# A transformer layer on one core: other scratch for block 2's squares, other slots for norms, late sums and output sums

## The chip, the cores and the metric

The kernel runs on one core of a Trainium2 chip. TensorE (PE) multiplies matrices and transposes, VectorE (DVE), ScalarE (ACT) and GpSimd (POOL) do the element work, and all transfers are issued from one queue, SyncE's (SP). The metric is the device time of one execution in microseconds; the median of several runs counts.

## The reference

The reference is one layer (`DEPTH` is 1, so only the first mixer runs) over a sequence of 2048 tokens of width 1024 in float32. The mixer is stick-breaking attention:

```python
def stick_breaking_mixer(h, w_qkv, w_o):
    qkv = (h @ w_qkv).reshape(b, s, 3, N_HEADS, HEAD_DIM)
    for q0 in range(0, s, SB_BLOCK):
        z = einsum('bthd,bshd->bhts', q[:, q0:end], k[:, :end]) * scale
        sp = where(mask, softplus(z), 0.0)
        rest = cumsum(sp, axis=3, reverse=True)
        a = exp(where(mask, z - rest, -inf))
        outs.append(einsum('bhts,bshd->bthd', a, v[:, :end]))
    return o @ w_o

def reference(x, c, ada_w, ada_b, norm_g, ffn_w_in, ffn_w_out, sb_w_qkv, sb_w_o, ...):
    mod_all = einsum('bd,lde->lbe', silu(c), ada_w) + ada_b[:, None]
    sh_m, sc_m, gt_m, sh_f, sc_f, gt_f = split(mod_all, 6)
    h = rms_norm(x, norm_g[0]) * (1 + sc_m) + sh_m
    x = x + gt_m * rms_norm(stick_breaking_mixer(h, ...), norm_g[1])
    h = rms_norm(x, norm_g[2]) * (1 + sc_f) + sh_f
    y = (silu(g) * u) @ ffn_w_out          # g, u = split(h @ ffn_w_in)
    return x + gt_f * rms_norm(y, norm_g[3])
```

The six vectors of `mod_all` are numbered 0 to 5 below (`seg`): shift, scale and gate of the mixer, then of the feed-forward part.

## The kernel before

**Numbers.** A float32 operand is split into a high part (rounded to a shorter format) and a low part (the rest), and a product is made of three matmuls (`mm3`, lines 190 to 194): high by high, high by low, low by high.

**Order.** The instructions of PE, ScalarE, VectorE and GpSimd run in the order in which the program writes them down. Transfers are put in order by the compiler's scheduler. All buffers come from pools with a fixed number of places under a tag: `ht` 5 (normed blocks), `qt` 3, `kt` 7, `v` 7, `wraw` 2, `qkn` 2, `tmp` 4; in PSUM `zps` 3 (scores), `tps` 2 (transposed weights), `accps` 3 under the tag `acc`. A new tile takes a place that is free, and its first writer waits until the last user of the place is done.

**Projections.** The tokens are four blocks of 512, the 16 heads eight pairs. A step (p, b) projects block b for head pair p: keys (t = 1), queries (t = 0), values (t = 2), each as eight slices over the width (k = 0 to 7), one slice being an `mm3`. `project(at)` is a generator that yields after each slice. `STEPS` begins with (0, 0), then (1, 0), whose results are parked in memory, then (0, 1), (0, 2), (0, 3), which are steps 2, 3 and 4. Steps 0 and 1 are computed ahead, in the lead-in written out by hand.

**Attention.** A unit is (pair, head, query block, key block), and each unit has four slots s. In every slot the program writes down one piece of each stage, with a delay in slots: scores `z` (line 588), sigmoids (605, 607), the scan that breaks the sticks (617, 622) and its product on GpSimd (629), the transposes `t` (639), their split into high (649) and low (655), the weighing of the values `o` (667), and some slices of the projections beside them. `project_to` sets how many: 18 slices are written before slot 0, and the projections then run ahead of the units.

**Norms of the first pair's blocks.** While head pair 0 is projected, each block is normed for the first time and stored for the other pairs. For block 2, `x_square` (line 328, through `rms_scale`, line 183) squares each of four tiles of 128 tokens on ScalarE and keeps only the sum; the squares themselves go to a scratch tile `xj` that nobody reads. `x_scale` (340) scales the rows on VectorE, `x_turn` (366) transposes them on PE, one eighth of the width at a time. Blocks 1 and 3 are loaded transposed (`xc`, line 325): `x_spread` and `x_share` bring the row factors into one tile, and `scale_cols` (376 on VectorE, 380 on GpSimd) multiplies by them. `modulate` then makes the high and the low part of a column tile (387 to 401). `first_norm(b, k)` does all this for eighth k of block b, and at odd k stores the finished pair (line 428). `X_AT` says in which slice the squares, scalings and loads are written; `NORM_AT` and the line below say the same for the norms:

```python
NORM_AT = [(2, 2), (2, 4), (2, 6)]      # eighths 0, 1, 2 of the next block, in the values product
first_norm(b, k + (4 if b == 1 else 3)) # the others, in the keys product of the block's own step
```

**Late modulation.** Segments 2 to 4 of `mod_all` are computed beside the attention by the generator `late_modulation`: from slot 120 on it is advanced every second slot. For each segment and each half it loads four chunks of weights into `wraw`, adds them up on VectorE (`aacc`), waits three steps (`settle`), takes an `acc` bank for the result `ap` and sums over the partitions on PE: one matmul by ones for a gate (line 293), four small products for a shift or scale (241). Three steps later (one for a shift or scale) VectorE reads the result (296, 249, 254). For a gate, a tile `gr` in `wraw` takes the constants (292) and goes out as rows (298). Segment 5 goes through the same function in the feed-forward part, with other tags.

**Output projection.** The two parts of each attention output are loaded (`o_load`), added (`o_add`, line 1082, on GpSimd for block 0 and on VectorE for the others) and split (`o_prep`). For block 0 this is written into the slots of the last pair.

The rest (output projection, second norm, feed-forward part) is not touched, but for segment 5 of the late modulation.

Of the kernel before, what the change touches and what calls it, by code (L numbers as in the profile page):

```python
# [9 lines left out]
F32 = mybir.dt.float32  # L10
F32R = mybir.dt.float32r
AF = mybir.ActivationFunctionType
ALU = mybir.AluOpType
# [3 lines left out]
P = 128  # L17
D = 1024
S = 2048
KC = D // P  # L20
# [3 lines left out]
BT = 512  # L24
# [26 lines left out]
BUFS = {  # L51
    "ht": 5, "whl": 4, "qt": 3, "kt": 7, "v": 7, "aT": 4, "qkn": 2, "wraw": 2,
    "tmp": 4, "w": 3, "a": 10,
}
# [35 lines left out]
    (3, 0, 1): [("share", 3)],  # L90
}

NORM_AT = [(2, 2), (2, 4), (2, 6)]

LAST_HELD = 30

# [24 lines left out]
def hybrid_trunk_kernel(  # L121
# [18 lines left out]
    nc = tc.nc  # L140
# [49 lines left out]
    def mm3(acc, lhs, rhs, first, last, **kw):  # L190

        nc.tensor.matmul(acc, lhs[0], rhs[0], start=first, stop=False, **kw)  # L192
        nc.tensor.matmul(acc, lhs[0], rhs[1], start=False, stop=False, **kw)  # L193
        nc.tensor.matmul(acc, lhs[1], rhs[0], start=False, stop=last, **kw)  # L194


    att = Places(ctx, tc)
    zps = ctx.enter_context(tc.tile_pool(name="zps", bufs=3, space=PSUM))
    tps = ctx.enter_context(tc.tile_pool(name="tps", bufs=2, space=PSUM))
    accps = ctx.enter_context(tc.tile_pool(name="accps", bufs=3, space=PSUM))  # L200
# [55 lines left out]
            g_eff[:, which, ks], sc, 1.0, gc[:, which, ks], op0=ALU.add, op1=ALU.mult  # L256
        )

    def late_modulation(segs, tag, n, ahead, waits, pool, ptag, acc_tag="tmp", rows_tag="wraw", settle=3, pace=1):

        chunks = [(seg, half, k0) for seg in segs for half in range(2) for k0 in range(0, KC, n)]
        loaded = []

        def load():
            if len(loaded) < len(chunks):
                loaded.append(ada_load(*chunks[len(loaded)], n, tag, BUFS[tag]))

        for _ in range(ahead):
            load()
        for at, (seg, half, k0) in enumerate(chunks):  # L270
            if ahead == 0 or at == 0:
                if ahead == 0:
                    load()
                for _ in range(waits):
                    yield
            if k0 == 0:
                acc = att.tile([P, BT], F32, name=f"aacc{seg}_{half}", tag=acc_tag, bufs=BUFS[acc_tag])
            for i in range(n):
                ada_add(acc, loaded[at], k0, i, k0 + i == 0)
                for _ in range(pace):  # L280
                    yield
            if ahead:
                load()
            if k0 + n < KC:
                continue
            for _ in range(settle):
                yield
            ps = pool.tile([P, BT], F32, name=f"ap{seg}_{half}", tag=ptag)
            if seg in (2, 5):
                g = seg // 3  # L290
                rows = att.tile([P, 2, BT], F32, name=f"gr{g}_{half}", tag=rows_tag, bufs=BUFS[rows_tag])
                nc.sync.dma_start(rows, gate_consts[g : g + 1, half].to_broadcast((P, 2, BT)))
                nc.tensor.matmul(ps, ones, acc, start=True, stop=True)
                for _ in range(3):
                    yield
                nc.vector.tensor_tensor(rows[:, 0], ps, rows[:, 0], op=ALU.add)
                nc.vector.tensor_tensor(rows[:, 0], rows[:, 0], rows[:, 1], op=ALU.mult)
                nc.sync.dma_start(gate_rows[g, :, half * BT : (half + 1) * BT], rows[:, 0])
            else:
                ada_cols([acc], ps, half)  # L300
                yield
                sl = slice(4 * half, 4 * half + 4)
                ada_done(seg, ps[:, sl], 1, sl)
            yield
# [3 lines left out]
    x_places = {}  # L308
# [19 lines left out]
    def x_square(b, i):  # L328
        junk = x_tiles[b, i]
        if b == 0:  # L330
            junk = x_norm[b, i] = att.tile([P, D], F32, name=f"xn{b}_{i}", tag="kt", bufs=BUFS["kt"])
        elif b == 2:
            junk = att.tile([P, D], F32, name=f"xj{b}_{i}", tag="wraw", bufs=BUFS["wraw"])
        x_rstd[b, i] = rms_scale(att, x_tiles[b, i], f"n0_{b}_{i}", junk=junk)

    def x_scale(b, i):
# [113 lines left out]
    def project(at):  # L450

        p, b = STEPS[at]
# [3 lines left out]
        nb = STEPS[at + 1][1] if at + 1 < len(STEPS) and STEPS[at + 1][0] == 0 else None  # L456
# [4 lines left out]
        def product(t):  # L461
            if begun:
                if at == 0 and t != 2:
                    first_norm(1, 2 + (t == 0))
                return first_acc[p, t]
            w = weights[p, t]
            acc = accps.tile([P, BT], F32, name=f"pj{p}_{b}_{t}", tag="acc")
            ahead = b == NB - 1 and p + 1 < NPAIR
            for k in range(KC):
                if t == 1:  # L470
                    if p == 0:
                        first_norm(b, k + (4 if b == 1 else 3))
                    if k in (3, 5) and waiting:
                        waiting.pop(0)()
                for what, *which in X_AT.get((at, t, k), []):
                    x_do[what](*which)
                if (t, k) in NORM_AT:
                    first_norm(nb, NORM_AT.index((t, k)))
                if ahead and k == 0:
                    load_weights(p + 1, t)  # L480
                if ahead and k == 6:
                    split_weights(p + 1, t)
                mm3(acc, (w[0][:, k], w[1][:, k]), (h[k][:, 0], h[k][:, 1]), k == 0, k == KC - 1)
                yield
            return acc

# [11 lines left out]
        n = split((yield from product(1)), "k")  # L498
# [13 lines left out]
        n = split((yield from product(0)), "q")  # L512
# [14 lines left out]
        acc = yield from product(2)  # L527
        tag = "w" if early else "tmp"
# [152 lines left out]
    rows, sums = {}, {}  # L681
# [267 lines left out]
    products(1, 6)  # L949
    products(0, 7)  # L950
    products(1, 7)
    late = late_modulation((2, 3, 4), "wraw", 2, 0, 3, accps, "acc")


    tasks = []
# [122 lines left out]
    def o_add(b, k):  # L1078
        parts = o_parts.pop((b, k))
        o = att.tile([P, BT], F32, name=f"of{b}_{k}", tag="tmp", bufs=BUFS["tmp"])  # L1080
        eng = nc.vector if b else nc.gpsimd
        eng.tensor_tensor(o, parts[:, 0], parts[:, 1], op=ALU.add)
        o_sum[b, k] = o

    def o_prep(b, k):
# [129 lines left out]
    for s in range(4 * len(units) + last):  # L1215
# [565 lines left out]
```

## Time and profile before

| what | value |
|---|---|
| median of 3 runs | 2841.5 us (2839.93 to 2845.77) |
| the profiled execution, its own time | 2840.45 us |
| its span from first to last instruction | 2838.2 us |
| mean granted TensorE clock | 0.998 |
| PE, VectorE, ScalarE, GpSimd busy | 2798.2, 2022.4, 1630.7, 1282.5 us |
| moved by DMA | 521.03 MB, mean 184 GB/s |

The span is what the profile's lines are measured in; the execution's own time is 2.25 us longer. Engines work in order, so an engine that waits holds up everything written down behind the waiting instruction. In a line of a timeline, the number in brackets is the idle time just before it, with what ended it. A granted clock of 1.00 is full speed of TensorE. In the lists of waits the numbers are the sum, the count and the longest.

### The profile page before, as it was taken

The numbers are of one execution on the slowest core, as the hardware profiler recorded it, in microseconds if no ns is written. First come the engines' busy times: TensorE is split into PE (matmuls) and PEld (weight loads), VectorE is DVE, ScalarE is ACT, GpSimd is POOL, SyncE is SP. The second block draws the span as 40 slices with busy tenths as digits, with TensorE's granted clock in tenths as the row PEclk, the third lists the DMA queues.
The fourth block names the chain that finished last, engine by engine and source line by source line (L and its number), as shares of the span: only waits on it lengthen the run. The fifth ranks groups of instructions, "written<-read, shape, count | busy, mean of one in ns | idle before, by whom it ended". The sixth has DMA issues, their size and how long they took to land.

```text
span 2838.2 us, 41766 instructions
## 1 busy us (share of the span) xinstructions
PE 2798.2 (99%) x13821; PEld 2331.5 (82%) x13821; DVE 2022.4 (71%) x2833; ACT 1630.7 (57%) x3271; POOL 1282.5 (45%) x2032
## 2 busy tenths in 40 slices
PE   9899999999999999999999999999999999999998
PEld 7688888888888888887888888888888888888887
DVE  7788888888888888888866766655775665123376
ACT  5787777787787877877645533333433333322243
POOL 1575666676576655657411222221222222544454
PEclk9999999999999999999999999999999999999999
DMA  9774556656665635546288644334453334545575
GB/s 378 275 226 164 186 163 220 212 179 226 193 210 187 214 115 178 196 134 231 85 304 308 207 138 152 123 94 160 137 178 108 112 108 164 192 140 155 180 226 187
DMA packets 239785, 521.03 MB, mean 184 GB/s; under 512 B 22481, under 2 KB 108497, under 8 KB 222674
## 3 DMA queue, kind: packets, MB, share of 16 engines
q1 hardware_dynamic: 239570, 518.38, 56.2%
q8 instruction: 109, 1.79, 0.3%
q14 instruction: 106, 0.87, 0.1%
HBM read 351.04 MB, written 118.49 MB: 165 GB/s over the span
## 4 chain that ended last, share of the span: by engine, by line
PE 88%; DVE 4%; issue 2%; DMA 2%; ACT 2%; POOL 1%; SPq 0%; DVEq 0%; POOLq 0%; ACTq 0%
PE s L192 9%; PE s L193 9%; PE s L194 9%; PE z L588 8%; PE o L667 8%; PE t L639 8%; PE pj L192 5%; PE pj L194 5%; PE pj L193 5%; PE o L194 5%; PE o L193 5%; PE o L192 5%; PE y L194 2%; PE y L192 2%; PE y L193 2%
## 5 line engine op out<-in xcount | busy, mean ns | idle before, releaser
L629 POOL TENSOR_TENSOR a<-a,w 128x512 f32<-128x512 f32 (+3 forms) x640 | 622.1, 972 | 218.9 <-DVE w L622 128.6
L622 DVE TENSOR_TENSOR_SCAN w<-z,c,begin 128x512 f32<-128x512 f32 x384 | 489.2, 1278 | 83.7 <-ACT z L607 62.0
L192 PE MATMUL s<-r,l 128*128 128x512 f32 x1232 | 481.4, 391 | 1.5 <-ACT p L1456 0.9
L194 PE MATMUL s<-r,l 128*128 128x512 f32 x1232 | 479.6, 389 | 0.0
L193 PE MATMUL s<-r,l 128*128 128x512 f32 x1232 | 479.4, 389 | 0.0
L605 ACT ACTIVATE a<-z 128x512 f32<-128x512 f32 (+3 forms) x640 | 347.1, 542 | 170.0 <-PE z L588 137.3
L667 PE MATMUL o<-aT,v 128*128 128x512 f32 (+3 forms) x1280 | 385.3, 382 | 0.1
L655 DVE TENSOR_TENSOR aT<-t,aT 128x512 fp32r<-128x512 f32 (+3 forms) x640 | 358.4, 593 | 24.3 <-ACT aT L649 23.7
L588 PE MATMUL z<-kt,qt 128*128 128x512 f32 (+3 forms) x1280 | 363.6, 365 | 0.0
L649 ACT CAST aT<-t 128x512 fp32r<-128x512 f32 (+3 forms) x640 | 313.9, 533 | 73.6 <-PE t L639 63.5
L607 ACT ACTIVATE z<-z 128x512 f32<-128x512 f32 (+3 forms) x640 | 344.8, 539 | 0.0
L1520 POOL TENSOR_TENSOR one<-p,p 128x512 f32<-128x512 f32 x44 | 70.6, 1606 | 574.5 <-issue 321.8
L192 PE MATMUL pj<-ht,w 128*128 128x512 f32 x768 | 309.3, 403 | 5.4 <-issue 1.4
L639 PE MATMUL t<-begin,a 128*128 128x128 f32 x2176 | 295.1, 273 | 13.3 <-DVE aT L655 12.0
L639 PEld LDWEIGHTS t<-begin,a 128*128 128x128 f32 x2176 | 255.2, 140 | 63.4 <-DVE aT L655 14.2
L193 PE MATMUL pj<-ht,w 128*128 128x512 f32 x768 | 301.7, 393 | 0.9 <-DVE ht L767 0.2
L194 PE MATMUL pj<-ht,w 128*128 128x512 f32 x768 | 301.9, 393 | 0.0
L192 PEld LDWEIGHTS s<-r,l 128*128 128x128 f32 x1232 | 231.2, 188 | 51.2 <-ACT p L1456 1.7
L194 PEld LDWEIGHTS s<-r,l 128*128 128x128 f32 x1232 | 231.2, 188 | 48.8 <-DVE l L1374 0.4
L193 PEld LDWEIGHTS s<-r,l 128*128 128x128 f32 x1232 | 231.3, 188 | 48.0 <-issue 0.5
L617 DVE TENSOR_TENSOR_SCAN w<-z,begin 128x128 f32<-128x128 f32 (+3 forms) x256 | 208.6, 817 | 76.9 <-ACT z L607 65.5
L588 PEld LDWEIGHTS z<-kt,qt 128*128 128x128 f32 x1280 | 230.9, 189 | 37.5 <-DVE w L617 0.2
(181 smaller groups left out, 4871.5 us busy)
## 6 DMA issues: line engine op xcount, KB each, us to landing
ht<-h_s SPq DMA_DIRECT2D x108, 1024.0 KB, 8.3
wi<-in_win SPq DMA_DIRECT2D x86, 512.0 KB, 3.9
qt<-qn SPq DMA_DIRECT2D x124, 256.0 KB, 4.8
ol_qt<-act_s SPq DMA_DIRECT2D x56, 512.0 KB, 3.7
act_s<-S SPq DMA_DIRECT2D x66, 256.0 KB, 4.0
br<-in_wout SPq DMA_DIRECT2D x66, 256.0 KB, 3.3
h_s<-ht SPq DMA_DIRECT2D x16, 1024.0 KB, 9.0
o_s<-os SPq DMA_DIRECT2D x128, 128.0 KB, 2.6
```

The source lines that it names most:

```text
L192: nc.tensor.matmul(acc, lhs[0], rhs[0], start=first, stop=False, **kw)
L193: nc.tensor.matmul(acc, lhs[0], rhs[1], start=False, stop=False, **kw)
L194: nc.tensor.matmul(acc, lhs[1], rhs[0], start=False, stop=last, **kw)
L588: nc.tensor.matmul(z[:, :n], q[:, e, part, r * P : (r + 1) * P], k[:, e, :n], start=part == 0, stop=part == 1,)
L605: nc.scalar.activation(a[:, :n], z[:, :n], AF.Sigmoid, scale=QK_SCALE)
L607: nc.scalar.activation(z[:, :n], z[:, :n], AF.Sigmoid, scale=-QK_SCALE)
L622: nc.vector.tensor_tensor_scan(rest[:, rev], left[:, rev], begin[:, :BT][:, rev], initial=carries[r], op0=ALU.mult, op1=ALU.bypass,)
L629: nc.gpsimd.tensor_tensor(a[:, :n], a[:, :n], rest[:, 1 : n + 1], op=ALU.mult)
L639: nc.tensor.transpose(pt[:, rb * P : (rb + 1) * P], weighed[i, rb][:, j * P : (j + 1) * P], ident)
L649: nc.scalar.copy(hl[:, 0, t0:], pt[:, t0:])
L655: nc.vector.tensor_tensor(hl[:, 1, t0:], pt[:, t0:], f32(hl[:, 0, t0:]), op=ALU.subtract)
L667: nc.tensor.matmul(acc[:, t0:], lhs, hl[:, part, t0:], start=sc == qb and j == 0 and part == 0, stop=sc == 0 and j == 3 and part == 1,)
```

## The change

Five edits. (1) The four squares of block 2 write to one tile under the tag `v`, taken at the first of them, in place of four tiles under `wraw`. (2) The norms of blocks 2 and 3 are written in other slices: the first in the queries product of the step before, then four in its values product, and the last three in the keys product of the block's own step. Block 1 keeps its slices. (3) Late sums: the result is made only when the last slice written is 2, 3 or 4 of its product (segments 2 to 4), and VectorE reads it in the same step. (4) The tile for a gate's rows and the transfer of its constants come before the settling steps. (5) The sums of block 0's output parts go from GpSimd to VectorE.

```diff
-NORM_AT = [(2, 2), (2, 4), (2, 6)]
+NORM_AT = {
+    None: [], 1: [],
+    2: [(0, 6), (2, 0), (2, 2), (2, 4), (2, 6)],
+    3: [(0, 4), (0, 7), (2, 2), (2, 4), (2, 6)],
+}
+
+NORM_IN_KEYS = {1: {0: 4, 1: 5, 2: 6, 3: 7}, 2: {0: 5, 1: 6, 3: 7}, 3: {0: 5, 1: 6, 3: 7}}
...
+    slice_at = [0]
...
-def late_modulation(..., settle=3, pace=1):
+def late_modulation(..., settle=3, pace=1, inside=None):
...
+            g = seg // 3
+            if seg in (2, 5):
+                rows = att.tile([P, 2, BT], F32, name=f"gr{g}_{half}", tag=rows_tag, bufs=BUFS[rows_tag])
+                nc.sync.dma_start(rows, gate_consts[g : g + 1, half].to_broadcast((P, 2, BT)))
             for _ in range(settle):
+                yield
+            while inside and slice_at[0] not in inside:
                 yield
             ps = pool.tile([P, BT], F32, name=f"ap{seg}_{half}", tag=ptag)
             if seg in (2, 5):
-                g = seg // 3
-                rows = att.tile([P, 2, BT], F32, name=f"gr{g}_{half}", tag=rows_tag, bufs=BUFS[rows_tag])
-                nc.sync.dma_start(rows, gate_consts[g : g + 1, half].to_broadcast((P, 2, BT)))
                 nc.tensor.matmul(ps, ones, acc, start=True, stop=True)
-                for _ in range(3):
-                    yield
                 nc.vector.tensor_tensor(rows[:, 0], ps, rows[:, 0], op=ALU.add)
...
             else:
                 ada_cols([acc], ps, half)
-                yield
                 sl = slice(4 * half, 4 * half + 4)
                 ada_done(seg, ps[:, sl], 1, sl)
...
         elif b == 2:
-            junk = att.tile([P, D], F32, name=f"xj{b}_{i}", tag="wraw", bufs=BUFS["wraw"])
+            if i == 0:
+                x_places["junk"] = att.tile([P, D], F32, name=f"xj{b}", tag="v", bufs=BUFS["v"])
+            junk = x_places["junk"]
...
                     if p == 0:
-                        first_norm(b, k + (4 if b == 1 else 3))
+                        first_norm(b, NORM_IN_KEYS[b].get(k, KC))
...
-                if (t, k) in NORM_AT:
-                    first_norm(nb, NORM_AT.index((t, k)))
+                if (t, k) in NORM_AT[nb]:
+                    first_norm(nb, NORM_AT[nb].index((t, k)))
...
                 mm3(acc, (w[0][:, k], w[1][:, k]), (h[k][:, 0], h[k][:, 1]), k == 0, k == KC - 1)
+                slice_at[0] = k
                 yield
...
-    late = late_modulation((2, 3, 4), "wraw", 2, 0, 3, accps, "acc")
+    late = late_modulation((2, 3, 4), "wraw", 2, 0, 3, accps, "acc", inside=range(2, 5))
...
-        eng = nc.vector if b else nc.gpsimd
-        eng.tensor_tensor(o, parts[:, 0], parts[:, 1], op=ALU.add)
+        nc.vector.tensor_tensor(o, parts[:, 0], parts[:, 1], op=ALU.add)
```

More of the change, by code (lines that the diff above doesn't have):

```diff
@@ L257, in ada_done, with late_modulation @@
         )
-    def late_modulation(segs, tag, n, ahead, waits, pool, ptag, acc_tag="tmp", rows_tag="wraw", settle=3, pace=1):
+    slice_at = [0]
+    def late_modulation(segs, tag, n, ahead, waits, pool, ptag, acc_tag="tmp", rows_tag="wraw", settle=3, pace=1, inside=None):
         chunks = [(seg, half, k0) for seg in segs for half in range(2) for k0 in range(0, KC, n)]
```

## The prediction

> **What bounds the kernel now.** I read the page first.
>
> ```profile
> span 2838.2 us, 41766 instructions
> PE 2798.2 (99%) x13821; PEld 2331.5 (82%) x13821; DVE 2022.4 (71%) x2833; ACT 1630.7 (57%) x3271; POOL 1282.5 (45%) x2032
> ```
>
> TensorE (PE) is the bound: it is busy for all but 40.0 us of the span, and the change takes no matmul away. So the only things to be had are idle time on PE and time in which it runs at a lower clock. I then looked for both where the edited code runs: PE's waits by window, and the granted clock by window.
>
> Slices are written (step, product, k) as in the code: one slice is three matmuls of a projection. Step 2 projects block 1, step 3 block 2, step 4 block 3, each in the order keys (1), queries (0), values (2). The first place is PE's timeline in step 2, from queries into values:
>
> ```profile
> 73.15 0.39 PE L194 MATMUL pj<-ht,w 128*128 128x512 f32 x1
> 73.38 0.33 PE L588 MATMUL z<-kt,qt 128*128 128x128 f32 x2
> 78.31 0.48 PE L366 MATMUL xT<-begin,x 128*128 128x128 f32 x1 [4.60 <-DVE x L340]
> ...
> 80.43 0.78 PE L192 MATMUL pj<-ht,w 128*128 128x512 f32 x1
> ...
> 83.14 1.05 PE L366 MATMUL xT<-begin,x 128*128 128x128 f32 x4
> 83.84 0.60 PE L192 MATMUL pj<-ht,w 128*128 128x512 f32 x1
> 84.28 0.40 PE L193 MATMUL pj<-ht,w 128*128 128x512 f32 x1
> ```
>
> Start to start, a matmul takes 0.23 us (73.15 to 73.38), so a slice is 0.68 us. PE ends the first scores at 73.71 (73.38 + 0.33) and then waits for the scaled rows of block 2, which it must transpose. From 80.43 on it runs at about half speed: six matmuls take 2.71 us to 83.14, and four transposes 0.70 us to 83.84. It is back to normal at 84.28. The work in between is two sets of transposes (0.35 each at full rate, half of 0.70) and seven matmuls (1.6), 2.3 us; it took 10.6 (73.71 to 84.28). **Loss here: 8.3 us.**
>
> Why the rows are late is seen in ScalarE's timeline, the SyncE queue's and the table of transfers:
>
> ```profile
> 64.03 0.56 ACT L540 CAST v<-vt 128x512 fp32r<-128x512 f32 x1
> 71.66 1.06 ACT L183 ACTIVATE xj<-x 128x1024 f32<-128x1024 f32 x1 [7.06 <-issue]
> ```
>
> ```profile
> 66.02 0.53 SPq L502 DMA_DIRECT2D k_park<-kn  x1
> ```
>
> ```profile
> k_park<-kn SPq DMA_DIRECT2D x1, 512.0 KB, 5.6
> ```
>
> ```profile
> 77.52 2.73 DVE L340 TENSOR_SCALAR x<-x,n_rstd 128x1024 f32<-128x1024 f32 x4
> ```
>
> The first square of block 2 writes its unused result into a `wraw` buffer. Both of these hold the parked keys and queries of step 1 until their copies land, and the first lands at 66.02 + 5.6 = 71.6: the square starts at 71.66. ScalarE works in order, so it stands still for 7.06 us with the split of step 2's keys behind it, and VectorE scales block 2's rows only from 77.52.
>
> The clock, by window. The windows are set to where it steps:
>
> ```profile
> 77.28:80.69 3.41, 1.81 (x5) 0.94 (x6) 3.41 (x6) 0.08 (x1) 0.05 (x2) 0.50 0.99 417
> 114.83:118.24 3.41, 1.99 (x10) 1.33 (x8) 3.28 (x5) 3.27 (x8) 3.32 (x4) 1.00 1.04 293
> 118.24:121.66 3.42, 3.24 (x21) 2.92 (x22) 2.60 (x4) 3.39 (x7) 2.94 (x4) 1.00 0.34 111
> 121.66:125.07 3.41, 1.17 (x7) 0.67 (x6) 3.41 (x6) 2.84 (x8) 3.33 (x4) 1.00 0.27 115
> 125.07:128.48 3.41, 3.37 (x12) 3.08 (x13) 2.70 (x5) 1.22 (x4) 2.32 (x8) 0.50 0.77 269
> ```
>
> First PE, then the other engines; the third number from the end is the granted clock. The wait from 73.71 to 78.31 is followed by a window at 0.50; one with PE busy for only 1.17 of 3.41 us (121.66) is too; one with 1.99 us busy (114.83) is not. A short stall is thus paid once, a longer one again in the next window, up to half of 3.41 us.
>
> **The change part by part.**
>
> *Scratch for the squares (gain 5.9 with the next edit).* The squares write into one `v` buffer. I count seven `v` buffers: two for the values of steps 0 and 1, four for block 3's rows, one left; the earlier holders were read before the square is due. So ScalarE starts at 64.59, at the end of the cast, 7.07 us earlier, and VectorE's scaling starts at 77.52 - 7.07 = 70.45. What is late next is PE's first transpose, since block 2's first norm moves from (2, 2, 2) to (2, 0, 6), four slices earlier: 73.38 - 4 x 0.68 = 70.65. Before, matmuls resumed 2.91 us after scaling began (77.52 to 80.43); now that is 73.36. Undisturbed it would be 71.0. The loss becomes 2.4 us in place of 8.3, in short pieces that leave PE busy for more than 1.99 us of a window, so at full clock. Gain 5.9. Ends: 8.3 (no wait at all) and -1.1 (ScalarE waits as before and PE, which asks 2.7 us earlier, stands from 70.65 + 0.35 to 80.43, 9.4 us).
>
> *Norms of blocks 2 and 3 spread.* The same sixteen norms, with all their transposes, casts, sums and stores, in other slots: two of each block go ahead of the values product. For block 3 this matters around 114 to 145, where PE waits for VectorE's split of the transposed weights:
>
> ```profile
> PE t L639 <- DVE aT L655: 5.9, 4, 2.3
> ```
>
> With the window at 0.50 (1.7 us of it lost) that is 7.6 us. The norm at (3, 2, 2), with two scalings on VectorE and one on GpSimd, goes to (3, 0, 4); the keys product of step 4 has three norms in place of five. I take the idle time of the window from 114.83 (1.4) as gone, the half clock (1.7) too, and a third of the other 4.5 (1.4): gain 4.5. Ends 0 and 7.6.
>
> [...]
>
> *What the moves take back (cost 2.0).* Earlier norms ask earlier for their data. Block 3's columns:
>
> ```profile
> L325 SPq DMA_DIRECT2D xc<-in_xt x4: 432/739/1193, 98.7 to 101.5; - x4
> L376 DVE SCALAR_TENSOR_TENSOR xc<-xc,g_eff,x x4: 727/736/1670, 113.9 to 135.1; 128x512 f32<-128x512 f32 x4
> ...
> DMA to landing us min/median/max: 6.2/6.6/7.9
> ```
>
> ```profile
> 105.53 0.39 PE L192 MATMUL pj<-ht,w 128*128 128x512 f32 x1
> ```
>
> They land between 104.9 (98.7 + 6.2) and 109.4 (101.5 + 7.9) and were first used at 113.9. Slice (3, 0, 4) is the one at 105.53, so VectorE will now ask about when they land, and in order behind that wait stand its scans and splits, for which PE's transposes wait. The DMA share, the number behind the clock, is 0.99 in the window from 77.28, so transfers may not move up as far as PE does; block 3's rows and the queries of step 2 are on the same queue. The stores of finished pairs move up on that queue with the norms. Ends: nothing, and all of the 5.9. I take 2.0, nearer to nothing, as the issue of the columns also moves up with PE.
>
> *Late sums.* Each of the six results for segments 2 to 4 takes one of three `acc` banks. PE's waits from 430 to 965:
>
> ```profile
> PE pj L192 <- issue: 1.4, 1, 1.4
> PE pj L192 <- DVE qn L491: 1.4, 1, 1.4
> ...
> PE pj L192 <- DVE kn L491: 0.9, 1, 0.9
> PE ap L293 <- DVE v L541: 0.7, 1, 0.7
> ...
> PE pj L192 <- DVE shift L249: 0.2, 1, 0.2
> PE pj L192 <- DVE gr L296: 0.2, 1, 0.2
> ```
>
> ```profile
> L293 PE MATMUL ap<-aacc,ones x8: 591/592/697, 431.9 to 2122.8; 128*128 128x512 f32 x8
> L296 DVE TENSOR_TENSOR gr<-ap,gr x4: 665/672/681, 446.1 to 2124.5; 128x512 f32<-128x512 f32 x4
> ```
>
> The first result is made at 431.9 and read at 446.1: a bank is held for 14 us, longer than a product, and a product that begins then must wait for the one before it to be split. These six waits come to 4.8 us. Now the result is read directly behind its matmul, and made in slices 2 to 4, when the former product's bank has been given back. Behind VectorE's new wait stand its scans; but the scan of the slot before already waits for scores that PE does later than most of that slot, so it should cost little. Gain 4.0; ends 4.8 and, if each of the six reads holds VectorE for a matmul's 0.6 us, -3.6.
>
> *Output sums on VectorE.*
>
> ```profile
> L1082 DVE TENSOR_TENSOR of<-op x12: 679/682/691, 1398.9 to 1437.5; 128x512 f32<-128x512 f32 x12
> L1082 POOL TENSOR_TENSOR of<-op x8: 1291/1506/1747, 1264.3 to 1334.6; 128x512 f32<-128x512 f32 x8
> ```
>
> ```profile
> 1335.85 0.66 PE L639 MATMUL t<-begin,a 128*128 128x128 f32 x4 [1.20 <-DVE aT L655]
> ```
>
> Eight sums go from 1.51 us each on GpSimd to 0.68 on VectorE, which adds 5.5 us to an engine that is busy for 71% of the span. One wait of 1.20 us follows the last of them. Gain 0.8; ends 1.2 and -5.5 (nothing covered).
>
> **Sum.** 5.9 + 4.5 - 2.0 + 4.0 + 0.8 = 13.2 us. The profiled execution took 2840.45, so 2827.3; the median of the runs, 2841.5, is 1.05 above it: **2828**.
>
> **The rivals.** *Transfers take it back (0.15).* PE gets to its data sooner than the queue delivers: the first place nets nothing, block 3's waits shrink by 1.0 only, and 4.0 + 0.8 stay: 5.8 us, 2836. For it speaks the DMA share of 0.99; against it, that no wait of PE between 60 and 430 names a transfer.
>
> *The scratch does not help (0.06).* Block 2's rows land late, or the `v` buffer is not free. ScalarE stands as long as before: -1.1 + 4.5 - 2.0 + 4.0 + 0.8 = 6.2, 2835. Against it: ScalarE's start at 71.66 fits the parked copy to 0.1 us.
>
> *The sums gain nothing (0.10).* The slice is looked at every second slot, so a result may still meet a product's start: 13.2 - 4.0 = 9.2, 2832.
>
> *Slower: the gate rows block the queue (0.10).* Their buffer is one of two in `wraw`, and it is now taken before the settling steps (three steps; three steps are the 14.2 us above) and kept through the wait for slice 2. The next pair's weights need the same two buffers on the same in-order queue, with the keys, queries and normed blocks of every step behind them. If a load of weights meets it, the queue stands up to 14 us, twice (two halves of segment 2): 28 - 9.2 = 19 slower, 2860. It decides once the queue stands for longer than the loads run ahead. Against it: the other buffer is free then, since the same generator loads nothing while it waits.
>
> **How the numbers follow.** The forecast case has 0.59. Its own range is 2822 (5.9 + 7.6 - 0 + 4.8 + 1.2 = 19.5 less) to 2834; with the first three rivals it reaches 2838. Left out are the slower case and the far end of the first rival, under 0.2. About 0.2%, 5.7 us, is what a measurement here can tell from no change: faster by more than that has 0.80 (the forecast, the sums' rival, most of the scratch's, half of the transfers'), within it 0.10, slower 0.10.
>
> **What would show it.** The first square right behind the cast, ScalarE idle there for under 1 us; PE's wait for block 2's rows under 1 us at its longest and no window at 0.50 between 75 and 85; none, or a shorter one, near 125; the t waits of 114 to 145 under 3 us in sum; a late result read within 4 us and no pj wait beside it; output sums at 0.68 to 0.7 us on VectorE. I am wrong if PE then waits for a transfer (qt, x, xc, wr) or VectorE stands for xc near 105, if t waits grow after 150, or if the half clock stays without a long wait before it.

## The result, and the profile after

| what | before | after |
|---|---|---|
| median of 17 runs each | 2840.70 us (2837.83 to 2845.77) | 2834.48 us (2829.92 to 2841.05) |
| ratio after to before | | 0.9975 [0.9968, 0.9982] |
| the profiled execution, its own time | 2840.45 us | 2831.56 us |
| its span | 2838.2 us | 2829.7 us |

The change makes the kernel about 7.1 us faster (0.0025 of 2840.7). The forecast was 13 us: the direction and the range hold, the size is half. The profiled execution of the changed kernel is 2.9 us below the median of its runs, so the traces show a little more gain (8.5 us of span) than the runs do.

The head of the page after: PE has the same number of instructions, and its idle time went from 40.0 to 33.7 us (2829.7 - 2796.0).

```profile
span 2829.7 us, 41799 instructions
...
PE 2796.0 (99%) x13821; PEld 2332.8 (82%) x13821; DVE 2032.7 (72%) x2841; ACT 1634.0 (58%) x3271; POOL 1269.9 (45%) x2024
```

**Where the time came from, by marks.** Both kernels compute the same scores in the same order, so the start of the first scores of a slot is a mark that can be compared between two traces. The table gives, for one execution of each kernel, its mark minus that of the kernel before (whose marks are at 99.87, 104.60, 146.19, 961.66, 1259.77 and 1342.05 us; the last scores start at 1388.48). The norms of block 2 that were moved lie ahead of slot 7 in both.

| kernel | slot 7 | slot 9 | slot 25 | slot 426 | slot 575 | slot 615 | last |
|---|---|---|---|---|---|---|---|
| after | -5.2 | -0.1 | -4.0 | -8.3 | -8.3 | -6.4 | -6.4 |
| scratch alone | -1.8 | -1.8 | -1.8 | -1.7 | -1.7 | -1.7 | -1.6 |
| norms alone | +0.8 | +1.1 | +4.3 | +4.7 | +4.7 | +4.7 | +4.7 |
| late sums alone | +3.0 | +3.0 | +3.1 | -1.4 | -1.4 | -1.4 | -1.4 |
| output sums alone | +0.5 | +0.5 | +0.6 | +0.6 | +0.6 | +2.4 | +2.5 |
| after, output sums of block 0 on GpSimd | -4.3 | -1.5 | -2.3 | -6.7 | -6.7 | -6.7 | -6.7 |
| after, block 2's norms in their old slices | -1.9 | -1.9 | -5.5 | -9.8 | -9.8 | -7.9 | -7.9 |
| after, own buffer for the queries, sums on GpSimd | -4.3 | -4.0 | -2.0 | -6.5 | -6.5 | -6.6 | -6.5 |
| after, three stores held back | -4.7 | -2.2 | -6.5 | -10.9 | -10.9 | -9.1 | -8.8 |
| the last two together | -5.2 | -4.9 | -10.0 | -14.4 | -14.3 | -14.4 | -14.3 |

Executions of one kernel reach slot 0 up to 6 us apart, because their lead-ins take differently long; this spread sits in the column of slot 7 ("late sums alone" shows it: nothing in it is changed that early). The kernels before and after entered the stretch together in these two traces: ScalarE's cast ahead of the first square starts at 64.03 and 64.04. The differences from one column to the next are free of it. In the line "after" they say: 5.2 us won at the first place, 5.1 lost again between slots 7 and 9, 3.9 won to slot 25, 4.3 won by the late sums to slot 426, 1.9 lost at the output sums.

**The first place.** ScalarE's timeline: the first square now begins inside the cast before it, where it had stood for 7.06 us.

```profile
64.04 0.56 ACT L551 CAST v<-vt 128x512 fp32r<-128x512 f32 x1
64.50 1.06 ACT L189 ACTIVATE xj<-x 128x1024 f32<-128x1024 f32 x1
```

PE's timeline there: four waits of at most 0.64 us for block 2's scaled rows in place of one of 4.60, then matmuls at 0.44 us from start to start in place of 0.23, which is half speed; the scores of slot 8 then wait 3.29 us for a transfer.

```profile
71.46 0.33 PE L376 MATMUL xT<-begin,x 128*128 128x128 f32 x1 [0.64 <-DVE x L350]
...
73.53 0.65 PE L198 MATMUL pj<-ht,w 128*128 128x512 f32 x1
73.97 0.63 PE L199 MATMUL pj<-ht,w 128*128 128x512 f32 x1
...
94.70 0.71 PE L599 MATMUL z<-kt,qt 128*128 128x512 f32 x2
...
100.06 0.41 PE L599 MATMUL z<-kt,qt 128*128 128x128 f32 x2 [3.29 <-DMA qt<-qn]
...
104.53 0.40 PE L599 MATMUL z<-kt,qt 128*128 128x256 f32 x2
```

**What took it back.** The SyncE queue (start, length of the group, transfer, count): behind the rows of block 3 (80.17) come two stores of block 2's finished pairs (85.82), 1 MB each, and then the queries of step 2 (90.13). The kernel before has the same order, but its two stores went out at 86.23 and 92.46.

```profile
80.17 5.55 SPq L327 DMA_DIRECT2D x<-in_x  x4
85.82 1.08 SPq L438 DMA_DIRECT2D h_s<-ht  x2
90.13 2.91 SPq L534 DMA_DIRECT2D qt<-qn  x4
93.14 1.30 SPq L438 DMA_DIRECT2D h_s<-ht  x1
94.49 7.29 SPq L333 DMA_DIRECT2D xc<-in_xt  x4
```

The queries were issued at 95.62 before. They are issued 5.5 us earlier now, but take 9.0 us to land and not 4.1. The tile's transfers between 70 and 110, after and then before:

```profile
DMA to landing us min/median/max: 8.8/9.0/9.3
```

```profile
DMA to landing us min/median/max: 3.2/4.1/4.9
```

So they land at about the same time as before (98.95 to 101.15 against 98.82 to 102.29), with the same rows and stores issued ahead of them, and all that PE had gained in front of them becomes a wait.

**The clock.** Windows of PE's clock (first PE's busy time, third from the end the granted clock). Three windows are still at 0.50, as many as before, where two followed the first place and one lay near 125:

```profile
70.27:73.68 3.41, 1.77 (x8) 0.78 (x7) 3.12 (x5) 0.00 (x0) 0.20 (x2) 1.00 1.04 432
73.68:77.09 3.41, 3.41 (x12) 2.75 (x12) 1.24 (x3) 1.37 (x2) 0.00 (x0) 0.50 1.00 418
97.58:100.99 3.41, 0.93 (x7) 0.93 (x8) 2.61 (x4) 1.21 (x3) 1.54 (x3) 1.00 1.04 317
100.99:104.40 3.41, 3.41 (x11) 2.71 (x10) 0.61 (x2) 1.31 (x4) 1.03 (x4) 0.50 0.99 383
121.47:124.88 3.41, 1.33 (x9) 0.97 (x7) 3.41 (x5) 1.93 (x7) 3.00 (x4) 1.00 0.77 282
124.88:128.29 3.41, 3.41 (x15) 3.09 (x14) 2.75 (x6) 2.01 (x5) 2.74 (x10) 0.50 0.59 197
```

The DMA share is about 1.0 through both stretches around the first two.

**Block 3.** PE's waits between 114 and 145 went from 5.9 us (4 of them) to 3.3:

```profile
PE t L650 <- DVE aT L666: 3.3, 3, 2.1
```

**Late sums.** PE's waits from 430 to 965: none for a projection's bank (`pj`) or for a late sum (`ap`) is left. The first result is made at 430.9 and read at 432.8, 1.9 us later, where it had been 14.2.

```profile
PE t L650 <- DVE aT L666: 2.6, 5, 0.7
PE t L650 <- POOL w L226: 0.6, 1, 0.6
```

```profile
L304 PE MATMUL ap<-aacc,ones x4: 590/592/592, 430.9 to 533.9; 128*128 128x512 f32 x4
L305 DVE TENSOR_TENSOR gr<-ap,gr x2: 666/667/668, 432.8 to 534.9; 128x512 f32<-128x512 f32 x2
```

**Output sums.** The group of the eight sums, then one of them on VectorE, what GpSimd does meanwhile, and PE behind it:

```profile
L1092 DVE TENSOR_TENSOR of<-op x8: 666/800/1468, 1254.7 to 1327.6; 128x512 f32<-128x512 f32 x8
```

```profile
1287.16 1.47 DVE L1092 TENSOR_TENSOR of<-op 128x512 f32<-128x512 f32 x1
1288.55 0.68 DVE L1100 TENSOR_TENSOR ohl<-of,ohl 128x512 fp32r<-128x512 f32 x1
1289.15 0.55 DVE L666 TENSOR_TENSOR aT<-t,aT 128x384 fp32r<-128x384 f32 x1
```

```profile
1286.99 1.10 POOL L640 TENSOR_TENSOR a<-a,w 128x512 f32<-128x512 f32 x1
```

```profile
1289.76 0.33 PE L650 MATMUL t<-begin,a 128*128 128x128 f32 x1 [1.19 <-DVE aT L666]
...
1330.01 0.66 PE L650 MATMUL t<-begin,a 128*128 128x128 f32 x4 [1.23 <-DVE aT L666]
```

A sum that begins while GpSimd multiplies takes up to 1.47 us and not 0.67, and the split behind it, for which PE waits, is late by that. Four of the eight sums began behind a product's start; they took 0.93, 1.12, 1.12 and 1.47 us, and each ended 0.55 us after the product did. The other four took 0.67. The wait of 1.20 us that the prediction wanted to remove is still there, with 1.23.

### The profile page after: what moved, and what is told of

The parts are those of the page before. It is cut to its first block, busy times and chain, and to the rows that moved or that the text cites. A ratio compares the mean times of both kernels' runs of the same rounds, so it can differ in the third digit from the quotient of the medians.

```text
span 2829.7 us, 41799 instructions
## 1 busy us (share of the span) xinstructions
PE 2796.0 (99%) x13821; PEld 2332.8 (82%) x13821; DVE 2032.7 (72%) x2841; ACT 1634.0 (58%) x3271; POOL 1269.9 (45%) x2024
## 4 chain that ended last, share of the span: by engine, by line
PE 87%; DVE 4%; DMA 3%; ACT 2%; issue 2%; POOL 1%; SPq 1%; DVEq 0%; POOLq 0%; ACTq 0%
PE s L198 10%; PE s L200 10%; PE s L199 10%; PE o L678 8%; PE z L599 8%; PE t L650 8%; PE pj L198 5%; PE pj L200 5%; PE pj L199 5%; PE o L198 4%; PE o L199 4%; PE o L200 4%; PE y L200 2%; PE y L198 2%; PE y L199 2%
```

## The experiments

All are compared with the kernel before on the same chip. First the four parts alone, each put into the kernel before.

**Scratch alone.**

```diff
-            junk = att.tile([P, D], F32, name=f"xj{b}_{i}", tag="wraw", bufs=BUFS["wraw"])
+            if i == 0:
+                x_places["junk"] = att.tile([P, D], F32, name=f"xj{b}", tag="v", bufs=BUFS["v"])
+            junk = x_places["junk"]
```

> The kernel before with the new scratch alone. Theory (transfers): the first square starts at 64.5 in place of 71.66, and since the transposes stay at slice (2, 2, 2), which PE reaches at 73.7 when the rows are scaled by 73.2, the wait and the half clock there go altogether: 8.3 us gained by slot 1. Of it 3 to 5 us are lost again at slot 8, where PE waits for the queries of step 2 (qt), because the queue gets no faster: net 3 to 5 us faster, 2836 to 2838. Rival (the spread norms made the wait for qt, by the stores that they move up): no wait for qt here, 8 us faster, 2832.

Measured: 2838.55 us against 2841.1, ratio 0.9993 [0.9984, 1.0002]: hardly a gain. The stall at the first place is gone (the mark of slot 1 stands at -6.9), and 6.1 us of it come back by slot 6, but not at the queries. ScalarE waits for the rows of block 3, and PE behind it for ScalarE:

```profile
88.41 1.06 ACT L183 ACTIVATE x<-x 128x1024 f32<-128x1024 f32 x1 [4.56 <-DMA x<-in_x]
```

```profile
91.27 1.11 PE L368 MATMUL xT<-begin,x 128*128 128x128 f32 x4 [4.65 <-ACT hf L389]
```

So removing the scratch's wait is worth nothing alone: the next transfer is waited for. Which one that is, I had wrong.

**Norms alone.**

```diff
-NORM_AT = [(2, 2), (2, 4), (2, 6)]
+NORM_AT = {
+    None: [], 1: [],
+    2: [(0, 6), (2, 0), (2, 2), (2, 4), (2, 6)],
+    3: [(0, 4), (0, 7), (2, 2), (2, 4), (2, 6)],
+}
+
+NORM_IN_KEYS = {1: {0: 4, 1: 5, 2: 6, 3: 7}, 2: {0: 5, 1: 6, 3: 7}, 3: {0: 5, 1: 6, 3: 7}}
...
```

So block 2 has one norm in the queries product and four in the values product, block 3 two and three.

> The kernel before with the spread norms alone, the scratch as before. Theory: ScalarE stands until 71.7 as before and PE, which now asks at 70.7, stands until 80.4, so 1 us is lost there; the qt wait stays away since PE is not early; from slot 9 to 25 the 3 to 4 us of block 3's norms are gained: 2 to 3 us faster in all, 2838. Rival (the spread pays only behind the scratch): no faster than before, 2841 or more.

Measured: 2846.8 us, ratio 1.0014 [1.0005, 1.0023]: slower, against my expectation. With ScalarE late, PE merely asks sooner and stands for longer, and then VectorE stands for block 3's columns, with PE behind it. PE, VectorE, PE:

```profile
77.89 0.48 PE L374 MATMUL xT<-begin,x 128*128 128x128 f32 x1 [6.95 <-DVE x L348]
```

```profile
112.84 2.52 DVE L384 SCALAR_TENSOR_TENSOR xc<-xc,g_eff,x 128x512 f32<-128x512 f32 x2 [6.03 <-DMA xc<-in_xt]
```

```profile
116.49 0.90 PE L648 MATMUL t<-begin,a 128*128 128x128 f32 x3 [6.45 <-DVE aT L664]
```

The wait of VectorE for the columns that the prediction feared is real here: slot 11 loses 7.2 us. After slot 12 the spread norms do win (from +10.0 back to +4.3 at slot 25).

**Late sums alone.** The edits (3) and (4).

```diff
+            while inside and slice_at[0] not in inside:
+                yield
             ps = pool.tile([P, BT], F32, name=f"ap{seg}_{half}", tag=ptag)
...
-                for _ in range(3):
-                    yield
...
+    late = late_modulation((2, 3, 4), "wraw", 2, 0, 3, accps, "acc", inside=range(2, 5))
```

> The kernel before with the late sums alone (made in slices 2 to 4, read at once, rows taken earlier). Theory: the six waits beside the results, 4.8 us, go; 0.5 to 1 us of t waits comes in: 4 us faster, 2837. Rival (the gate rows hold a buffer and block the queue): t or pj waits near 420 to 480 of more than 3 us and no gain.

Measured: 2837.48 us, ratio 0.9988 [0.9980, 0.9997]: 3.4 us faster. Between slots 25 and 426 it wins 4.5 us (3.05 to -1.43), as the whole change does there (4.3). This part stands by itself.

**Output sums alone.**

```diff
-        eng = nc.vector if b else nc.gpsimd
-        eng.tensor_tensor(o, parts[:, 0], parts[:, 1], op=ALU.add)
+        nc.vector.tensor_tensor(o, parts[:, 0], parts[:, 1], op=ALU.add)
```

> The kernel before with the output sums alone on VectorE. Theory (the sums collide with GpSimd's products and push the split of the transposed weights back): sums of 1.2 to 1.5 us where GpSimd works, t waits between 1255 and 1300 grow by 2 us, 1 to 2 us slower, 2842 to 2843. Rival (the prediction): sums of 0.7 us, 0.8 us faster.

Measured: 2842.33 us, ratio 1.0007 [0.9998, 1.0016]; the time alone doesn't tell it from none. The marks do: nothing anywhere but 1.85 us lost between slots 575 and 615, and PE's waits for the split between 1240 and 1350 us rise from 3.2 (first line, the kernel before) to 5.5 us (second line):

```profile
PE t L639 <- DVE aT L655: 3.2, 5, 1.2
PE t L639 <- DVE aT L655: 5.5, 6, 1.2
```

Then versions of the changed kernel.

**Output sums back on GpSimd.** The last diff reversed.

> The changed kernel with block 0's output sums back on GpSimd. Theory (the sums collide on VectorE): the 1.9 us lost between slots 581 and 615 come back: 2 us under the changed kernel, 2832. Rival: the loss there has another cause (the shift in time of everything before) and stays: 2834.

Measured: 2834.8 us, ratio 0.9976 [0.9966, 0.9985], the same as the change itself. Between slots 575 and 615 nothing is lost now (in place of 1.9), but in this execution VectorE waits 3.4 us for block 3's columns, and slot 11 gives back 3.4. Up to slot 575 this version does the same as the changed kernel, so that wait is a difference between two executions and not between two kernels. The edit is undone where it acts; in the total it is lost in what executions differ by.

**A buffer of its own for the queries of step 2.**

```diff
-            qt = att.tile([P, 2, 2, BT], F32R, name=f"qt{p}_{b}", tag="qt", bufs=BUFS["qt"])
+            place = "whl" if at == 2 else "qt"
+            qt = att.tile([P, 2, 2, BT], F32R, name=f"qt{p}_{b}", tag=place, bufs=BUFS[place])
```

> The changed kernel with the queries of step 2 in a buffer of another tag (whl), so that they need not wait for the transposes of block 2. Theory (the queue's order and the wait for a buffer make PE's 3.3 us wait at slot 8 and the half clock behind it): the queries go out near 86 in place of 90.1 and PE waits there for under 1 us; 3 to 5 us faster than the changed kernel, 2830 to 2831. Rival (the transfers themselves are the bound, whatever their order): the wait moves to block 3's columns on VectorE (xc) and to t waits near 100 to 108, and slot 9 is no earlier than 1 us before that of the changed kernel.

Measured: 2834.12 us, ratio 0.9973 [0.9963, 0.9982]. The queries are issued at 85.2 in place of 90.1, and PE's wait of 3.3 us for them is gone, with the half clock behind it (4.8 us to slot 9). Slot 11 gives 3.3 of it back: VectorE waits for the columns. The time is that of the changed kernel, and not the 2830 to 2831 expected.

```profile
104.56 2.52 DVE L386 SCALAR_TENSOR_TENSOR xc<-xc,g_eff,x 128x512 f32<-128x512 f32 x2 [2.69 <-DMA xc<-in_xt]
```

**Both of these.**

> Both of these together: the queries of step 2 in another buffer and the output sums on GpSimd. By the theories 5 to 7 us under the changed kernel, 2828 to 2830; by the rivals as the changed kernel, 2834.

Measured: 2831.29 us, ratio 0.9966 [0.9953, 0.9979]. Again the queries cost nothing, and the columns cost more in this execution (up to slot 575 it does the same as the last version): 5.4 us at slot 11 and 1.1 at slot 12. VectorE, PE, and when the tile's transfers landed:

```profile
105.94 2.51 DVE L386 SCALAR_TENSOR_TENSOR xc<-xc,g_eff,x 128x512 f32<-128x512 f32 x2 [4.28 <-DMA xc<-in_xt]
```

```profile
109.59 0.90 PE L651 MATMUL t<-begin,a 128*128 128x128 f32 x3 [4.68 <-DVE aT L667]
```

```profile
DMA to landing us min/median/max: 11.3/12.2/12.3
```

**Block 2's norms in their old slices, block 3's spread.**

```diff
-    2: [(0, 6), (2, 0), (2, 2), (2, 4), (2, 6)],
+    2: [(2, 2), (2, 4), (2, 6)],
...
-NORM_IN_KEYS = {1: {0: 4, 1: 5, 2: 6, 3: 7}, 2: {0: 5, 1: 6, 3: 7}, 3: {0: 5, 1: 6, 3: 7}}
+NORM_IN_KEYS = {1: {0: 4, 1: 5, 2: 6, 3: 7}, 2: {0: 3, 1: 4, 2: 5, 3: 6, 4: 7}, 3: {0: 5, 1: 6, 3: 7}}
```

> The changed kernel with block 2's norms at their old slices; block 3's stay spread. Theory (transfers bound the stretch from 80 to 105): as with the scratch alone, ScalarE waits 4 to 5 us for block 3's rows and PE for a transpose behind it, so slot 7 is 1 to 2 us ahead of the kernel before in place of 5.2, and the wait for qt is small: by slot 9 the two orders come out within 1 us of each other, and the whole within 2 us of the changed kernel, 2833 to 2836. Rival (the spread of block 2's norms is what made the qt wait): 4 us faster than the changed kernel, 2830.

Measured: 2828.83 us, ratio 0.9959 [0.9945, 0.9972]. The wait for the queries is gone, and block 3's rows are late instead, as with the scratch alone; the half clock stays behind it. By the marks the two orders are 1.8 us apart at slot 9, where the theory said within 1 us; the time is under the rival's 2830, but the next version shows how little that decides.

```profile
88.06 1.06 ACT L189 ACTIVATE x<-x 128x1024 f32<-128x1024 f32 x1 [4.11 <-DMA x<-in_x]
```

**The same, with the output sums on GpSimd.**

> The changed kernel with block 2's norms at their old slices and block 0's output sums on GpSimd. Theory: the two edits that cost or gain nothing are out, so the 1.9 us of the sums come on top of the kernel with block 2's norms put back alone (2828.8): 2827. Rival (that kernel's 1.5 us lead over the changed one was chance): 2832, as the changed kernel with the sums on GpSimd.

Measured: 2832.36 us, ratio 0.9966 [0.9956, 0.9976]; I had expected 2827. The output sums cost nothing again (1.9 us less than in the last version between slots 575 and 615), but this execution reached slot 0 6.1 us later: 10.2 us of its lead-in (23.67 to 33.91) ran at a granted clock of 0.50, which the last version's did not (mean clock of the execution 0.996 against 0.998). The lead of the last version over this one is therefore no effect of an edit that I can name; the two intervals overlap.

**And block 3's rows loaded two slices earlier**, at (2, 1, 6) and not (2, 0, 0).

```diff
-    (2, 1, 6): [("square", 2, 2)],
+    (2, 1, 6): [("square", 2, 2), ("load", 3)],
...
-    (2, 0, 0): [("scale", 2, 0), ("load", 3)],
+    (2, 0, 0): [("scale", 2, 0)],
```

> The same, with the load of block 3's rows written at slice (2, 1, 6), so that the queue issues it ahead of the keys of step 2, 5 us earlier. Theory (this stretch is bound by the order and the mass of the transfers): ScalarE's 4.1 us wait for block 3's rows and PE's 4.2 us behind it go, with the half clock; a part comes back as a wait for the keys or queries of step 2 (kt, qt) or for block 3's columns, since the same bytes must go: 0 to 4 us faster than the kernel without the early load, 2824 to 2828. Rival (the wait is ScalarE's own order, not the transfers'): the same wait stays.

Measured: 2832.34 us, ratio 0.9968 [0.9955, 0.9980]. The wait for the rows falls from 3.4 to 1.6 us, slot 6 starts 3.1 us earlier after slot 0 (against the last version), and slots 11 and 12 lose 3.6 again, to the columns:

```profile
108.85 2.54 DVE L386 SCALAR_TENSOR_TENSOR xc<-xc,g_eff,x 128x512 f32<-128x512 f32 x2 [2.33 <-DMA xc<-in_xt]
```

All of these that touch this stretch show the same: whatever transfer is helped, another is waited for. If it is the amount to be moved between 66 and 106 us that binds, taking bytes out of that stretch must help where an earlier issue doesn't.

**Three stores held back.** The changed kernel, with the first three stores of block 2's pairs (3 MB), which nobody reads soon, written at (3, 0, 4).

```diff
+            elif b == 2 and k < 6:
+                held_2.append(out_of)
...
+                if (at, t, k) == (3, 0, 4):
+                    for out_of in held_2:
+                        nc.sync.dma_start(*out_of)
```

> The changed kernel, with the first three stores of block 2's finished pairs (1 MB each, two of them on the queue ahead of the queries of step 2) held back until slice (3, 0, 4). Nothing else differs; all work is done. If the transfers as such bound the stretch from 66 to 105 us (share of the 16 DMA engines about 1.0, some 375 GB/s, so 2.8 us for each MB): the queries of step 2 land 4 to 6 us after issue in place of 9.0, PE's wait for them goes from 3.3 to 0.5 us at most, the window at half clock behind it goes, block 3's columns land in 7 us or less with no new wait of VectorE for them, slot 9 starts 4 to 5 us earlier, and the time is 2829 to 2831. If it is the release of the buffer of the queries that makes them late (issue at 90.1, four slots earlier impossible), the wait stays at 2.5 us or more and the time at 2834. If the three stores then fall on other loads, the gain at slot 9 is given back between slots 11 and 25.

Measured: 2828.78 us, ratio 0.9960 [0.9948, 0.9973]. The queue and PE's timeline:

```profile
80.19 6.05 SPq L327 DMA_DIRECT2D x<-in_x  x4
86.29 1.61 SPq L333 DMA_DIRECT2D xc<-in_xt  x3
90.31 2.66 SPq L539 DMA_DIRECT2D qt<-qn  x4
```

```profile
99.52 0.41 PE L604 MATMUL z<-kt,qt 128*128 128x128 f32 x2 [2.27 <-DVE aT L671]
```

The time came out as for the theory of the bytes, and nothing waits for the columns, which took 9.6 us and not under 7 to land, but three of the four were issued 8 us earlier; the half clock near 101 is gone. The queries did not come out: three loads of the columns (1.5 MB) moved into the place of the stores (2 MB), ahead of the queries, whose issue still waits until 90.31 for a buffer; they landed in 8.8 us, and slot 8 still stands for 2.27. The profile puts this wait down to VectorE, but the queue of PE's weight loads stood at a semaphore until 99.35, and the second of the four loads of the queries landed at 99.32. Both the buffer and the bytes count, so next both are removed.

**The same stores held back, own buffer for the queries, sums on GpSimd.**

> The same stores held back, in the version with the queries of step 2 in a buffer of their own kind and block 0's output sums on GpSimd (median 2831.3). All work is done. If transfers bound the stretch, block 3's columns land 11 to 12 us after issue there only for the bytes ahead of them: with 3 MB less they land in 8 us or less, the 5.3 us lost at slot 11 shrinks to 2 or less, and the time is 2827 to 2828. If the columns are late because of where their load is issued, slot 11 keeps its loss and the time stays at 2831.

Measured: 2827.8 us (2824.30 to 2829.96), ratio 0.9954 [0.9941, 0.9968]. The queue:

```profile
80.35 5.15 SPq L327 DMA_DIRECT2D x<-in_x  x4
85.59 2.77 SPq L540 DMA_DIRECT2D qt<-qn  x4
88.40 4.97 SPq L333 DMA_DIRECT2D xc<-in_xt  x4
```

The columns are issued at 88.40 and not at 94.62 as without the held stores, and land in 9.8 us and not 12.2 (8 or less was expected); no wait for a transfer between 66 and 150 is longer than 0.5 us, and against that version's execution slots 11 and 12 win 6.5 us. This version beats both kernels: by 13 us the one before, and by 6 the changed one (0.9975 less 0.9954 of 2840.7; their intervals against the kernel before meet at 0.9968). Against the same version without the held stores (0.9966) it is 3.4 us faster, and the two intervals overlap.

## Why the prediction was right, and where it was not

**Scratch (predicted gain 5.9): right, but not to keep.** ScalarE began at 64.50 (64.59 forecast), and the mark of slot 7 moved by 5.2. The waits inside were as named (0.64 at the longest). What failed is the step "in short pieces that leave PE busy for more than 1.99 us of a window, so at full clock": the window had 1.77 us of work and the next was at 0.50.

**"What the moves take back" (2.0, nearer to nothing): this is the step that failed.** It measured 5.1, nearly its far end, and the transfer waited for was the queries, not the columns for which the term was worked out. The sentence that the DMA share of 0.99 may not let transfers move up as far as PE was on record, and so was the rival in which "the first place nets nothing"; I gave that too little weight with the reason that no wait of PE named a transfer. That reason is empty when PE's own stalls are what covers the transfers. The stretch from 66 to 106 moves data at a share of about 1.0 (0.96 to 1.02 in steps of 10 us); the windows after show it even where PE idles:

```profile
86.00:96.00 10.00, 9.66 (x54) 7.72 (x53) 8.65 (x18) 9.41 (x21) 5.55 (x12) 1.00 0.99 385
96.00:106.00 10.00, 6.71 (x29) 5.29 (x28) 5.95 (x10) 4.10 (x11) 4.18 (x11) 0.83 1.02 357
```

The runs show this by interference: rows of block 3 (scratch alone, old slices), queries (the change), columns (norms alone, own buffer, earlier rows) are waited for in turn, and taking 3 MB out of the stretch, with the own buffer, ended these waits (0.5 us at most is left). How much that is worth is less sure: 7.8 us by the last mark of two executions (-6.5 to -14.3, of which 0.9 was there at slot 7), 3.4 by the ratios of the runs, and 4.3 by the ratios for the held stores in the changed kernel (0.9975 to 0.9960); in both pairs the intervals overlap.

**Norms of block 3 (4.5): right in size, wrong in one item.** 3.9 by the marks, 2.6 of it in PE's waits. The half clock near 125 that I took as gone stayed in the changed kernel, so whether it comes from these waits at all has to be looked at. In the best version the same three waits are there (0.35, 2.08 and 0.84 us), and the clock stays full behind them; only the first line, early in the stretch, is followed by half clock (73.98 to 77.40):

```profile
70.57:73.98 3.41, 1.78 (x7) 0.78 (x6) 2.96 (x5) 0.03 (x1) 0.03 (x1) 1.00 1.03 429
...
114.94:118.36 3.42, 1.76 (x11) 1.29 (x9) 3.42 (x5) 3.15 (x9) 3.36 (x3) 1.00 0.99 289
118.36:121.77 3.41, 2.88 (x18) 2.14 (x18) 3.15 (x7) 1.99 (x6) 2.92 (x8) 1.00 1.00 380
```

The wait of 2.08 us (116.70 to 118.78) straddles an edge between two windows here and left 1.76 us of work in the first; in the changed kernel it lay inside one (121.65 to 123.73 in 121.47 to 124.88), left 1.33, and the next window was at half clock. The version with block 2's norms in their old slices and the sums on GpSimd agrees: its wait of 2.07 us (125.77 to 127.84) straddles an edge at 126.07, and the clock stays full. So it is these waits, and where they fall. In the changed kernel the clock stepped at 73.68, 77.09, 100.99, 104.40, 124.88 and 128.29, each a whole multiple of 3.41 us from the next (one, seven, one, six and one); that edges lie at such multiples also where the clock does not step is my estimate from these steps. A gap of 2.08 us cost a window at half clock in the changed kernel and none in the best version. In this best version block 3's part is worth 5.2.

**Late sums (4.0): right.** 4.3 in the change, 4.5 alone, 4.1 to 4.5 in every version that has them, and no wait of a projection beside them. PE's waits for the split rose there from 1.2 to 2.6 us, the price of VectorE's reads. The slower rival, the gate rows blocking the queue, did not happen: from 430 to 965 neither PE nor VectorE nor ScalarE waits for a transfer.

**Output sums (gain 0.8): wrong in sign.** They cost 1.9, between the ends on record (1.2 and -5.5). The step that failed is the price: "0.68 on VectorE" was taken from rows where GpSimd was not multiplying beside them. The median was 0.80 and the longest 1.47, and PE waits for the split behind them. The four slow sums took 2.0 us more than 0.67 each in all, and each stands, with the splits behind it, right ahead of one of PE's waits (0.71, 0.93, 1.19 and 1.23 us). My estimate from these rows is that at 0.67 the waits there would have come to 3.5 us, near the 3.2 of before: no loss, but no gain of 0.8 either, as VectorE's own work takes the place of the wait for GpSimd. In the trace the four sums that began behind the start of a product on GpSimd took 0.93 to 1.47 us and the other four 0.67, and the four slow ones ended 0.55 us after the product, whatever their start; what holds them up there was not shown.

**The sum.** With the transfers and the output sums out of the way, the best version wins 4.9 at slot 9, 5.2 to slot 25 and 4.4 to slot 426, together 14.4. The three terms on record for these are 5.9, 4.5 and 4.0, also 14.4. That the sums agree to the tenth is luck, since one term is 1.0 too large and the others 0.7 and 0.4 too small, and this version differs from the change in three edits; but each gain was sized to about 1 us, and the forecast missed by the two costs.

**The number.** The time, 2834.48, is nearer to the first rival (2836) than to the forecast (2828), and just outside the forecast's own range to 2834; it lies in the stated range because that reaches to the rivals. Of the rival's two items the first came true (the first place netted 0.1), and the second did not (block 3's waits shrank by 2.6, not 1.0).

**What stays open.** The parts alone do not add up to the change (-2.6 + 5.7 - 3.6 + 1.2 = 0.7 slower by the medians, against 6.2 faster for all together). The norms lose where the scratch still holds ScalarE back, so the two need each other; by how much each order of edits would pay was not separated. Executions reach slot 0 up to 6 us apart, and the three with the longest lead-ins ran 10 to 17 us of them at half clock (late sums alone from 19.67 to 33.32 us; the other two are the versions with block 2's norms in their old slices and the sums on GpSimd; the mean clocks of these three executions are 0.996, 0.996 and 0.995, those of the others 0.997 to 0.999); why the clock was low there was not tried. The versions between 0.9954 and 0.9968 overlap in their intervals.

## What to carry to other kernels

When the DMA share of a stretch stands at 1.0, ask whether PE's stalls there are the cover under which transfers land: here each stall that was removed came back at the next transfer (5.2 us won and 5.1 lost in the change), though no wait of PE had named a transfer before. Look in such a stretch for bytes that nobody needs soon (here stores) before looking for an earlier issue. And a price for an operation moved between VectorE and GpSimd has to be read from rows in which the other engine is busy as it will be (here 0.67 us alone, up to 1.47 behind a product's start).

## What the runs showed of the hardware

- The same transfer of 256 KB took 4.1 us from issue to landing in one trace and 9.0 in the other, with the same transfers ahead of it on the queue and the DMA share at 0.88 to 1.02 in both (86 to 106 us); the earlier issue hardly landed earlier (5.5 us earlier in issue; the first load landed 0.1 us later, the last 1.1 us earlier).
- A granted clock of 0.50 followed windows with PE busy for 0.93, 1.17, 1.33, 1.77 to 1.81 and in one trace 2.08 of 3.41 us (late sums alone, 81.11 to 84.52); windows with 1.64 (126.07 to 129.48, in the version with the old slices and the sums on GpSimd), 1.76 and 1.99 us were followed by full clock. So the profile's busy time alone does not decide between 1.6 and 2.1 us, and one wait of 2.08 us cost a window at half clock or none, by where it fell.
- An addition of two 128x512 tiles took 0.67 us on VectorE, and 0.93 to 1.47 when a product on GpSimd had begun before it; it then ended 0.55 us after the product. Where the addition began first, it took 0.67, and in two cases the product behind it 1.39 in place of 1.09.
